# The Newton step of single-column inverse roots on GpSimd, and an output product that asks for no new weights

## The chip, the cores and the metric

The kernel runs on one core of a Trainium2 chip. The metric is the device time of one execution in microseconds (us); lower is better. Engines are called as in the profile: PE (TensorE matmuls), PEld (its weight loads), DVE (VectorE), ACT (ScalarE), POOL (GpSimd), SP (SyncE, which issues the DMAs here).

## The reference

Three blocks run one after the other on a sequence of 1024 positions of width 1024, all in float32: an attention block with a learned choice of 256 keys, a block of gated linear attention (GLA: 4 heads, head width 512 on the value side, chunks of 64), and a block with a state space model (S5), a gate and an output product; a last RMS norm ends it. What bears on this case is the inverse root of each norm, and the GLA head's way to the output:

```python
def _rmsnorm(x, g):
    y = x32 * lax.rsqrt(jnp.mean(x32 * x32, axis=-1, keepdims=True) + EPS) * g
...
    o = o_intra + jnp.einsum('bhncd,bhnde->bhnce', q_g, s_prev)
    o = o.transpose(0, 2, 3, 1, 4).reshape(bsz, seqlen, GLA_HEADS, GLA_DV)
    o = o * lax.rsqrt(jnp.mean(o * o, axis=-1, keepdims=True) + EPS) * head_gain.astype(f32)
    o = o.reshape(bsz, seqlen, D_INNER) * jax.nn.silu(z.astype(f32))
    return o.astype(h.dtype) @ w_out
```

## The kernel before, in words

All matmuls are float32 made of three products of "hi" and "lo" parts: `mm3` (lines 192 to 196) issues hi·hi, hi·lo and lo·hi into the same PSUM bank. Weights come from DRAM as raw pieces of 512 KB and are **split** on the chip: ACT casts the hi part (line 179), and DVE or POOL subtracts to get the lo part (line 187). A class `WStream` keeps the order: `put` lists the pieces, `pump(n)` splits up to n of the next ones, if the ring of six split pieces has room (`released + RING`) and if the raw piece's load was issued at least `age` pumps ago; `ahead` issues the loads of up to three raw pieces; `take(ids)` gives split pieces to a product, and splits at once, whatever the age, those that are not split yet; `release` gives ring places back.

**The inverse root.** `G.rsqrt` (line 204) takes a column of sums of squares. With up to four columns POOL makes v = mean + eps (line 211) and h = v to the power -0.5 (line 212); then one Newton step of four small DVE instructions (lines 215 to 218) gives the result. With `later=True` the Newton step is returned as a function, and the caller issues it some steps on. The single-column callers are: the norm of each of 8 row blocks at the end of the attention block (line 1325), each of the 32 items of the GLA core (line 1971), the 8 norms of the GLA result (line 2008), and the 8 last norms (`finish`, line 2447). The two calls with four columns, at the start, and those with more are not of this kind.

**The GLA core** (lines 2066 to 2089) goes through 32 items: 4 heads with 8 tiles of 128 positions each. Each item is a generator (`core`, line 1942) of five parts, and one turn of the loop, called a **round** here, advances the items under way in the order written in `turn` (line 2060), so that the instructions of a round stand in this order in every engine's queue:

1. the part 4 of item n-2: four PE transposes of y (line 1977) into a PSUM bank, ACT copy to hi (1982), DVE subtraction to lo (1983);
2. part 2 of item n-1: PE product with the state of the items before, DVE y = product times gate (1969), ACT squares with their sum (1970), POOL power (211, 212);
3. part 1 of item n: PE products, DVE new state `Sf` (1957), ACT `Shi` (1960), POOL `Slo` (1961 by line 187); the state is used by PE two rounds later;
4. part 3 of item n-1: the Newton step on DVE;
5. part 5 of item n-3: the output product, 24 matmuls of 512 columns with the head's four weight pieces (1992) into two banks, and then two DVE additions into `xacc` (1998), which multiply by the inverse root.

After that come two steps of `prep_unit`, which makes queries, keys and masks for the next four items; among its instructions are four PE transposes and 24 short matmuls (1920, 1930) in one round of four, an ACT copy and a POOL mask (1933). The round then ends with `ws.pump(1)` (line 2086). The name `mm` in the profile stands for four PSUM banks handed out in turn, so the transposes of the next round wait for a bank that the additions of line 1998 give back.

In a head's last tile (`last`, line 1989) the output product goes through the four weight pieces one after the other for both banks, releases each piece behind its use, and calls `ws.pump` there (line 1995): that puts the splits of the next pieces into the queues of ACT and DVE ahead of the additions of line 1998. A head's first tile takes its four pieces (line 1986) before its output product.

**The end of the kernel.** For each of the last four row blocks (lines 2530 to 2545): DVE adds the product, ACT squares, DVE adds two sums (2446), `rsqrt`, DVE scales twice (2450), and SP stores.

Of the kernel before, what the change touches and what calls it, by code (L numbers as in the profile page):

```python
# [16 lines left out]
OP = mybir.AluOpType  # L17
# [17 lines left out]
def f32(ap):  # L35
    return ap.bitcast(F)
# [110 lines left out]
class G:  # L147
# [56 lines left out]
    def rsqrt(self, pool, out, ssq, n, scale, later=False):  # L204

        nc = self.nc
        v = pool.tile([P, n], F, name=f"rs_v{n}", bufs=2 if n == 1 else 1)
        h = pool.tile([P, n], F, name=f"rs_h{n}", bufs=2 if n == 1 else 1)
        t = pool.tile([P, n], F, name=f"rs_t{n}", bufs=2 if n == 1 else 1)
        if n <= 4:  # L210
            nc.gpsimd.tensor_scalar(v, ssq, scale, EPS, op0=OP.mult, op1=OP.add)
            nc.gpsimd.tensor_tensor(h, v, self.mhalf[:, :n], OP.pow)  # L212

            def newton():
                nc.vector.tensor_tensor(t, h, h, OP.mult)  # L215
                nc.vector.tensor_tensor(t, t, v, OP.mult)  # L216
                nc.vector.scalar_tensor_tensor(t, t, -3.0, h, op0=OP.add, op1=OP.mult)
                nc.vector.tensor_scalar(out, t, -0.5, None, op0=OP.mult)
            return newton if later else newton()
        nc.vector.tensor_scalar(v, ssq, scale, EPS, op0=OP.mult, op1=OP.add)  # L220
        nc.vector.tensor_scalar(h.bitcast(I32), v.bitcast(I32), 1, None, op0=OP.logical_shift_right)
        nc.vector.tensor_scalar(out.bitcast(I32), h.bitcast(I32), -1.0, float(0x5F3759DF - 0x80000000),
                                op0=OP.mult, op1=OP.add)
        nc.vector.tensor_scalar(h, v, 0.5, None, op0=OP.mult)
        for _ in range(3):
            nc.vector.tensor_tensor(t, out, out, OP.mult)
            nc.vector.tensor_tensor(t, t, h, OP.mult)
            nc.vector.scalar_tensor_tensor(out, t, -1.5, out, op0=OP.add, op1=OP.mult)
# [1490 lines left out]
def gla(g, xn2, xstack, prep):  # L1719
    nc, tc, A, ws = g.nc, g.tc, g.A, g.ws  # L1720
# [221 lines left out]
    def core(h, st, v, z):  # L1942
        u = res[h, st // 4]
        p = st % 4
        sl = slice(p * P, (p + 1) * P)
        pk = g.big() if st < NST - 1 else None
        po = g.big()
        before = st8.get("S")
        if st < NST - 1:
            g.mm3(pk, [a[:, sl] for a in u["ke"]], v, True, True)  # L1950
        g.mm3(po, [a[:, sl] for a in u["am"]], v, True, st == 0)
        if st < NST - 1:
            Sf = wk2.tile([P, 512], F, name="Sf")
            if st == 0:
                nc.vector.tensor_copy(Sf, pk)
            else:
                nc.vector.scalar_tensor_tensor(Sf, before[0], u["dS"][:, p:p + 1], pk, op0=OP.mult, op1=OP.add)
            Shi = wk2.tile([P, 512], R, name="Shi")
            Slo = wk2.tile([P, 512], R, name="Slo")
            nc.scalar.copy(Shi, Sf)  # L1960
            g.sub("pool", Slo, Sf, f32(Shi))
            st8["S"] = (Sf, Shi, Slo)
        yield
        if st > 0:
            g.mm3(po, [a[:, sl] for a in u["qp"]], before[1:], False, True)
        ssq = wk2.tile([P, 1], F, name="ssq")
        rst = wk2.tile([P, 1], F, name="rsh", bufs=4)
        y = wk2.tile([P, 512], F, name="y")
        nc.vector.tensor_tensor(y, po, z, OP.mult)
        nc.scalar.activation(wk2.tile([P, 512], BF, name="sq", bufs=1), po, AF.Square, accum_out=ssq)  # L1970
        newton = g.rsqrt(wk2, rst, ssq, 1, 1.0 / 512, True)
        yield
        newton()
        yield
        ps = g.bank()
        for j in range(4):
            nc.tensor.transpose(ps[:, j * P:(j + 1) * P], y[:, j * P:(j + 1) * P], g.ident)
        wk2.tile([P, 32], F, name="ypad", bufs=1)
        yh = wk2.tile([P, 4, P], R, name="yh")
        yl = wk2.tile([P, 4, P], R, name="yl")  # L1980
        pv_ = ps.rearrange("p (a b) -> p a b", a=4)
        nc.scalar.copy(yh, pv_)
        nc.vector.tensor_tensor(yl, pv_, f32(yh), OP.subtract)
        yield
        if st == 0:
            st8["W"] = ws.take(pwo[h])
        ps = [g.bank(), g.bank()]
        cols = [slice(nh * 512, nh * 512 + 512) for nh in range(2)]
        last = st == NST - 1
        for i in range(8):  # L1990
            nh, j = (i % 2, i // 2) if last else (i // 4, i % 4)
            g.mm3(ps[nh], (yh[:, j], yl[:, j]), [a[:, 0, cols[nh]] for a in st8["W"][j]], j == 0, j == 3)
            if last and nh:
                ws.release(pwo[h][j:j + 1])
                ws.pump(j < 3)
        for nh in range(2):
            xs = xacc[:, st, cols[nh]]
            nc.vector.scalar_tensor_tensor(xs, ps[nh], rst, xs, op0=OP.mult, op1=OP.add)  # L1998
        if h == 3:
            nc.sync.dma_start(g.x3_d[st * P:(st + 1) * P, :], xacc[:, st, :])  # L2000
            norms.append(norm(st))
# [3 lines left out]
    def norm(st):  # L2005
        ss = g.small.tile([P, 2], F, name="nss", bufs=3)
        nc.scalar.activation(g.junk(), xacc[:, st, :], AF.Square, accum_out=ss[:, 0:1])
        newton = g.rsqrt(g.small, ss[:, 1:2], ss[:, 0:1], 1, 1.0 / D, True)
        yield
        yield  # L2010
        newton()
        yield
        nc.vector.tensor_scalar(xacc[:, st, :], xacc[:, st, :], ss[:, 1:2], None, op0=OP.mult)
# [52 lines left out]
    for n, (h, st) in enumerate(items):  # L2066
        if st % 4 == 0:
            for _ in pg:
                pass
            ui = n // 4 + 1  # L2070
            pg = pgs.pop(n, iter(()))
            if 0 < n and ui < len(units):
                pg = prep_unit(*units[ui], st8["next"])
        gens[n] = core(h, st, vs.pop(n), vz.pop(n)[1])
        if n + 1 < len(items):
            vs[n + 1] = split_v(vz[n + 1][0], "pool" if n % 2 else "dve")
        turn(n)
        next(pg, None)
        if n < 8 and n % 2 == 0:
            nc.sync.dma_start(xacc[:, n:n + 2], g.x2_d[n * P:(n + 2) * P].rearrange("(t p) d -> p t d", p=P))  # L2080
        if n + 3 < len(items):
            vz[n + 3] = load_vz(*items[n + 3])
        next(pg, None)
        if st % 4 == 1 and ui + 1 < len(units):
            st8["next"] = load(*units[ui + 1])
        ws.pump(1)
# [518 lines left out]
```

## Time and profile before

| | |
|---|---|
| median of 3 runs | 2616.41 us (2616.41 to 2618.24) |
| the profiled execution | 2615.66 us, span 2613.9 us, mean granted clock 0.964 |
| PE busy | 2417.1 us, 92% of the span |
| DVE busy | 1708.2 us, 65% |
| ACT busy | 1109.5 us, 42% |
| POOL busy | 1127.5 us, 43% |

The page gives busy time by engine, the span in forty slices, the chain of work that ended last, and groups of instructions by line. Times are counted from the first instruction. A bracket at the end of a row of the order in time, such as [5.55 <-DVE xacc L1998], is the engine's idle time before that instruction and what ended it. PE's busy time is modelled from pipelined matmuls; the distance between the starts of two matmuls is the better measure of its pace.

### The profile page before, as it was taken

The page shows a single profiled execution, that of the slowest core. Times are in us where ns is not written, and L with a number is a line of the kernel's source. Part 1 is how long each engine was busy: PE and PEld are TensorE (multiplying, and loading weights), DVE is VectorE, ACT ScalarE, POOL GpSimd, SP SyncE. Part 2 cuts the span into 40 slices and gives each one's busy share as a digit, 9 for nine tenths or more (in the row PEclk, how much of TensorE's full clock was granted, in tenths as well). Part 3 has the DMA queues.
Part 4 walks back from the last instruction along what each step waited for, and adds up shares of the span by engine and source line. Part 5 has one row for each costly group of instructions (what it writes and reads, how often), then busy time and mean ns, then how long its engine had stood idle before and what let it go on. Part 6 is the DMA issues. An engine that isn't in the chain of part 4 may idle for free.

```text
span 2613.9 us, 33041 instructions
## 1 busy us (share of the span) xinstructions
PE 2417.1 (92%) x11817; PEld 1990.4 (76%) x11817; DVE 1708.2 (65%) x3015; ACT 1109.5 (42%) x1812; POOL 1127.5 (43%) x826
## 2 busy tenths in 40 slices
PE   5787977999999999999989899999999899999998
PEld 4665755777777777777777678888888788888887
DVE  5889887777454556785777770389788555425642
ACT  5455683656532122324443443444443533323331
POOL 3517465322211566664444424555554433333431
PEclk8998988999999999999989899999999899999999
DMA  8302124221332645535432316777554644444441
GB/s 263 113 30 62 54 87 154 85 65 56 107 122 84 159 136 152 165 122 177 153 113 85 93 69 164 194 202 201 183 154 146 192 133 121 149 139 146 140 149 57
DMA packets 330173, 338.25 MB, mean 129 GB/s; under 512 B 67366, under 2 KB 248182, under 8 KB 329752
## 3 DMA queue, kind: packets, MB, share of 16 engines
q1 hardware_dynamic: 330008, 336.13, 42.2%
q8 instruction: 93, 1.52, 0.2%
q14 instruction: 72, 0.59, 0.1%
HBM read 239.19 MB, written 96.87 MB: 129 GB/s over the span
## 4 chain that ended last, share of the span: by engine, by line
PE 30%; DVE 10%; issue 5%; DMA 3%; POOL 3%; ACT 2%; SPq 0%; POOLq 0%; DVEq 0%; ACTq 0%
PE mm L194 8%; PE mm L196 8%; PE mm L195 8%; PE big L196 2%; PE big L195 2%; PE big L194 2%; POOL whl L187 2%; DMA w<-syp_d 2%; DVE xacc L1998 1%; DVE X L2326 1%; DVE rs_t L215 1%; DVE mm L2257 1%; POOL rs_h L212 1%; DVE mm L2255 1%; DVE rs_t L216 1%
## 5 line engine op out<-in xcount | busy, mean ns | idle before, releaser
L187 POOL TENSOR_TENSOR whl<-wraw,whl 128x1024 fp32r<-128x1024 f32 x183 | 443.3, 2431 | 606.0 <-ACT whl L179 527.3
L179 ACT CAST whl<-wraw 128x1024 fp32r<-128x1024 f32 (+1 forms) x279 | 288.5, 1048 | 360.9 <-PE mm L196 220.0
L194 PE MATMUL mm<-h_hi,whl 128*128 128x512 f32 x768 | 308.0, 401 | 14.5 <-DVE gT L952 7.8
L196 PE MATMUL mm<-h_hi,whl 128*128 128x512 f32 x768 | 302.0, 393 | 0.0
L195 PE MATMUL mm<-h_lo,whl 128*128 128x512 f32 x768 | 301.4, 392 | 0.0
L194 PE MATMUL mm<-whl,h_hi 128*128 128x512 f32 (+1 forms) x720 | 288.4, 400 | 13.0 <-ACT whl L179 9.6
L195 PE MATMUL mm<-whl,h_hi 128*128 128x512 f32 (+1 forms) x720 | 282.1, 392 | 10.8 <-DVE whl L187 10.8
L196 PE MATMUL mm<-whl,h_lo 128*128 128x512 f32 (+1 forms) x720 | 281.1, 390 | 0.0
L187 DVE TENSOR_TENSOR whl<-wraw,whl 128x1024 fp32r<-128x1024 f32 (+2 forms) x96 | 133.4, 1399 | 147.2 <-ACT whl L179 147.1
L194 PE MATMUL mm<-y_hl,whl 128*128 128x512 f32 x512 | 201.3, 393 | 0.0
L195 PE MATMUL mm<-y_hl,whl 128*128 128x512 f32 x512 | 199.9, 390 | 0.0
L196 PE MATMUL mm<-y_hl,whl 128*128 128x512 f32 x512 | 199.8, 390 | 0.0
L194 PEld LDWEIGHTS mm<-h_hi,whl 128*128 128x128 f32 x768 | 146.0, 190 | 49.5 <-DVE gT L952 8.7
L196 PEld LDWEIGHTS mm<-h_hi,whl 128*128 128x128 f32 x768 | 145.5, 189 | 32.2
L195 PEld LDWEIGHTS mm<-h_lo,whl 128*128 128x128 f32 x768 | 146.1, 190 | 29.4 <-issue 0.5
L194 PEld LDWEIGHTS mm<-whl,h_hi 128*128 128x128 f32 x720 | 137.7, 191 | 40.4 <-ACT whl L179 10.1
L195 PEld LDWEIGHTS mm<-whl,h_hi 128*128 128x128 f32 x720 | 138.0, 192 | 36.9 <-DVE whl L187 12.2
L196 PEld LDWEIGHTS mm<-whl,h_lo 128*128 128x128 f32 x720 | 137.3, 191 | 28.5
L187 POOL TENSOR_TENSOR w<-w 128x512 f32<-128x512 f32 x32 | 55.1, 1722 | 168.2 <-ACT w L2434 168.2
L196 PEld LDWEIGHTS mm<-y_hl,whl 128*128 128x128 f32 x512 | 96.5, 189 | 20.1
L194 PEld LDWEIGHTS mm<-y_hl,whl 128*128 128x128 f32 x512 | 97.0, 189 | 19.4
L195 PEld LDWEIGHTS mm<-y_hl,whl 128*128 128x128 f32 x512 | 96.6, 189 | 19.5
(542 smaller groups left out, 5928.8 us busy)
## 6 DMA issues: line engine op xcount, KB each, us to landing
wraw<-in_s_w_glu_dram SPq DMA_DIRECT2D x64, 512.0 KB, 3.9
wraw<-in_gla_w_in_dram SPq DMA_DIRECT2D x40, 512.0 KB, 4.3
wraw<-in_s_w_in_dram SPq DMA_DIRECT2D x32, 512.0 KB, 5.6
wraw<-in_s_w_out_dram SPq DMA_DIRECT2D x32, 512.0 KB, 3.6
gv_d<-stg SPq DMA_DIRECT2D x32, 256.0 KB, 2.2
v_mat<-vc SPq DMA_DIRECT2D x32, 256.0 KB, 2.6
w_mat<-wo SPq DMA_DIRECT2D x32, 256.0 KB, 2.5
gz_d<-stg SPq DMA_DIRECT2D x32, 256.0 KB, 2.1
```

The costliest lines, as they stand in the source:

```text
L179: nc.scalar.copy(out, in_)
L187: e.tensor_tensor(out, a, b, op)
L194: nc.tensor.matmul(out, lhsT=lhs[0], rhs=rhs[0], start=start, stop=False)
L195: nc.tensor.matmul(out, lhsT=lhs[0], rhs=rhs[1], start=False, stop=False)
L196: nc.tensor.matmul(out, lhsT=lhs[1], rhs=rhs[0], start=False, stop=stop)
L212: nc.gpsimd.tensor_tensor(h, v, self.mhalf[:, :n], OP.pow)
L215: nc.vector.tensor_tensor(t, h, h, OP.mult)
L216: nc.vector.tensor_tensor(t, t, v, OP.mult)
L1998: nc.vector.scalar_tensor_tensor(xs, ps[nh], rst, xs, op0=OP.mult, op1=OP.add)
L2255: nc.vector.tensor_tensor(a, x, wide(L[0], n), OP.mult)
L2257: nc.vector.tensor_tensor(c[half[q]], x[half[1 - q]], wide(L[1][half[1 - q]], n), OP.mult)
L2326: nc.vector.tensor_tensor(Xo.rearrange("p (g o) t -> p g t o", g=8), gto(parts.pop(o)), gto(ps), OP.add)
```

## The change

Two edits. In `rsqrt`, with one column, the Newton step is issued on POOL right behind the power, with four instructions (`h*h`, times v, times -0.5 plus 1.5, times h), and the function handed back does nothing. The formula is the same. In the last tile of a head the product no longer calls `ws.pump`; it still releases the pieces.

```diff
@@ -210,6 +210,12 @@
         if n <= 4:
             nc.gpsimd.tensor_scalar(v, ssq, scale, EPS, op0=OP.mult, op1=OP.add)
             nc.gpsimd.tensor_tensor(h, v, self.mhalf[:, :n], OP.pow)
+            if n == 1:
+                nc.gpsimd.tensor_tensor(t, h, h, OP.mult)
+                nc.gpsimd.tensor_tensor(t, t, v, OP.mult)
+                nc.gpsimd.tensor_scalar(t, t, -0.5, 1.5, op0=OP.mult, op1=OP.add)
+                nc.gpsimd.tensor_tensor(out, t, h, OP.mult)
+                return lambda: None
 
             def newton():
                 nc.vector.tensor_tensor(t, h, h, OP.mult)
@@ -1992,7 +1998,6 @@
             g.mm3(ps[nh], (yh[:, j], yl[:, j]), [a[:, 0, cols[nh]] for a in st8["W"][j]], j == 0, j == 3)
             if last and nh:
                 ws.release(pwo[h][j:j + 1])
-                ws.pump(j < 3)
         for nh in range(2):
             xs = xacc[:, st, cols[nh]]
             nc.vector.scalar_tensor_tensor(xs, ps[nh], rst, xs, op0=OP.mult, op1=OP.add)
```

## Rows read from the trace of the kernel before

**Rows 1.** Windows: length, then busy us (count) by engine, PEclk, DMA share, GB/s

```profile
1238.93:1553.72 314.79, 280.87 (x1311) 232.00 (x1311) 230.10 (x390) 125.14 (x246) 133.56 (x160) 0.92 0.32 105
1320.00:1325.00 5.00, 0.00 (x0) 0.00 (x0) 4.90 (x8) 2.92 (x5) 2.75 (x3) 0.69 0.74 227
1325.00:1330.00 5.00, 4.62 (x16) 3.88 (x17) 3.68 (x6) 1.51 (x4) 1.33 (x3) 0.63 0.77 267
```

**Rows 2.** Groups by line, 1235 to 1560: busy us, mean ns | idle before, releaser

```profile
L215 DVE TENSOR_TENSOR rs_t<-rs_h 128x1 f32<-128x1 f32 x40 | 28.8, 721 | 33.0 <-POOL rs_h L212 32.8
L216 DVE TENSOR_TENSOR rs_t<-rs_t,rs_v 128x1 f32<-128x1 f32 x40 | 18.6, 465 | 1.4
L217 DVE SCALAR_TENSOR_TENSOR rs_t<-rs_t,rs_h 128x1 f32<-128x1 f32 x40 | 16.6, 414 | 1.4
```

**Rows 3.** Waits, 1235 to 1560: us in total, times, longest

```profile
PE mm L1977 <- DVE xacc L1998: 22.7, 6, 6.1
```

**Rows 4.** PE in order of time: start, us, line, tiles, count, [idle before]

```profile
1308.30 0.60 PE L1977 MATMUL mm<-ident,y 128*128 128x128 f32 x4
...
1316.63 0.60 PE L1920 MATMUL mm<-ident,ek 128*128 128x128 f32 x4
...
1319.55 0.28 PE L196 MATMUL mm<-qgh,kkl 128*128 128x64 f32 x1
1325.38 1.12 PE L1977 MATMUL mm<-ident,y 128*128 128x128 f32 x4 [5.55 <-DVE xacc L1998]
...
1334.96 0.60 PE L1977 MATMUL mm<-ident,y 128*128 128x128 f32 x4
...
1342.92 0.60 PE L1977 MATMUL mm<-ident,y 128*128 128x128 f32 x4
...
1350.87 0.60 PE L1977 MATMUL mm<-ident,y 128*128 128x128 f32 x4
...
1365.07 1.11 PE L1977 MATMUL mm<-ident,y 128*128 128x128 f32 x4 [2.25 <-DVE xacc L1998]
...
1374.53 0.60 PE L1977 MATMUL mm<-ident,y 128*128 128x128 f32 x4
```

**Rows 5.** POOL and DVE in order of time at a head's last tile

```profile
1318.96 1.27 POOL L187 TENSOR_TENSOR Slo<-Sf,Shi 128x512 fp32r<-128x512 f32 x1
...
1319.02 1.22 DVE L215 TENSOR_TENSOR rs_t<-rs_h 128x1 f32<-128x1 f32 x1 [1.08 <-POOL rs_h L212]
...
1320.74 3.93 DVE L187 TENSOR_TENSOR whl<-wraw,whl 128x1024 fp32r<-128x1024 f32 x3
1324.59 1.40 DVE L1998 SCALAR_TENSOR_TENSOR xacc<-mm,rsh,xacc 128x512 f32<-128x512 f32 x2
```

**Rows 6.** ACT and DVE in order of time, around splits in other rounds

```profile
1339.00 0.62 ACT L1960 CAST Shi<-Sf 128x512 fp32r<-128x512 f32 x1
...
1346.78 1.05 ACT L179 CAST whl<-wraw 128x1024 fp32r<-128x1024 f32 x1
...
1347.86 1.47 DVE L187 TENSOR_TENSOR whl<-wraw,whl 128x1024 fp32r<-128x1024 f32 x1 [0.78 <-ACT whl L179]
```

**Rows 7.** POOL in order of time: first and last of another four-instruction Newton step

```profile
421.70 0.29 POOL L1043 TENSOR_TENSOR qrt<-qrs 128x64 f32<-128x64 f32 x1
...
422.82 0.33 POOL L1046 TENSOR_TENSOR qrs<-qrs,qrt 128x64 f32<-128x64 f32 x1
```

**Rows 8.** POOL and DVE in order of time, the last finish

```profile
2608.01 0.19 POOL L211 TENSOR_SCALAR rs_v<-fss 128x1 f32<-128x1 f32 x1 [4.69 <-DVE fss L2446]
2608.28 0.55 POOL L212 TENSOR_TENSOR rs_h<-rs_v,mhalf 128x1 f32<-128x1 f32 x1
...
2609.64 1.42 DVE L2450 SCALAR_TENSOR_TENSOR x<-x,frs,fn 128x512 f32<-128x512 f32 x2
```

**Rows 9.** POOL and DVE in order of time, end of the GLA stage

```profile
1549.46 2.35 POOL L187 TENSOR_TENSOR whl<-wraw,whl 128x1024 fp32r<-128x1024 f32 x1
...
1549.58 2.25 DVE L216 TENSOR_TENSOR rs_t<-rs_t,rs_v 128x1 f32<-128x1 f32 x1
```

## The prediction, made before the change was built

> **What bounds the kernel now.** PE is busy 92% of the span, so a change on DVE, POOL and ACT can only pay where PE stands still or runs at the lower clock. I read the windows first, to find such places. In the GLA core, 314.8 us long, PE is busy 280.9 us and the mean granted clock is 0.92 [rows 1]. The loss is not spread: in 1320 to 1325 PE does nothing, and the next 5 us run at a granted clock of 0.63, that is for much of the time at 1.2 instead of 2.4 GHz [rows 1]. The view of waits says what PE stood for: the transposes of line 1977 waited 22.7 us in six stops for DVE's additions into `xacc` [rows 3], which give their PSUM bank back. Then I read PE in order of time, round by round [rows 4]. A round without a stop lasts 1350.87 - 1342.92 = 7.95 us. In one round of four the short products of `prep_unit` come on top, from 1316.63 to about 1319.66, 3.0 us, so that round should last 10.95 us. At the end of a head it lasted 1325.38 - 1308.30 = 17.08 us, 6.13 too long, and the round behind it 9.58 us, 1.63 too long, because its first part ran at the low clock. In the middle of a head the same two rounds lasted 14.20 and 9.46 us, so 3.25 and 1.51 are lost [rows 4]. Each kind occurs three times: 3 x 7.76 = 23.3 us at the ends of heads, 3 x 4.76 = 14.3 us in the middles.
>
> Why are the additions late? The groups by line show that the small Newton instructions do not cost their 0.16 us here: the three with two inputs take 0.72, 0.47 and 0.41 us on average, and DVE stands idle another 33.0 us ahead of them for POOL's power [rows 2]. In order of time the reason is to be seen: line 215 begins at 1319.02, behind POOL's `Slo` that began at 1318.96, and ends when `Slo` ends [rows 5]. At the end of a head, idle time and Newton step hold DVE from 1317.94 to 1320.74, 2.8 us, and then three splits hold it to 1324.59; only then come the additions, and PE goes on at 1325.38 [rows 5, 4].
>
> **The Newton step leaves DVE.** In the core it takes 28.8 + 18.6 + 16.6 us of DVE and 33.0 us of waiting in 40 calls [rows 2], some 2.4 us a round. With it gone, the additions come right behind `Sf`, or when the product ends. In the middle of a head PE's transposes waited 2.25 us for them [rows 4], less than the 2.8 us of idle time and Newton step ahead of the additions at the head's end [rows 5], and the rounds before lag less as well. I take these three stops as gone: -14.3 us. Less than all is bounded by the DVE work that stays; none of it gone would be 0.
>
> On POOL the same step costs this: another Newton step there, with 64 columns, took 421.70 to 423.15, 1.45 us, 0.29 to 0.33 us for an instruction with two inputs [rows 7]. With one column a POOL instruction is 0.19 us and the next begins 0.27 us after it [rows 8], so four take 0.08 + 3 x 0.27 + 0.19 = 1.08 us. That is the value I take; 1.5 us is the upper end, and the 0.81 us that DVE needs from the end of the power to line 2450 [rows 8] the lower. POOL is busy 133.6 of 314.8 us in the core [rows 1], 4.2 us a round; 5.3 fits into 7.95. Queued behind the step on POOL are `Slo`, the mask and the lo parts of v. `Slo` is used two rounds later, the inverse root two rounds later, the mask a round later, so 1.08 us is hidden. Only the first mask of the stage has no such slack; there I add 1.1 us (0 to 1.5).
>
> The Trainium skill, page "GPSIMD Engine Reference", section 4.1 "Engine selection", advises against this edit: adding and multiplying belongs on VectorE, since GpSimd is about twice as slow with two inputs. By it each of the three such instructions would take 2 x 0.16 = 0.32 us instead of 0.19, an estimate from that page, and a finish would lose 0.4 us more. The rows with one and with 64 columns are 0.19 and about 0.3 us [rows 7, 8], so the start of an instruction sets the time and I keep to the rows. The Trainium skill's page "SBUF — State Buffer", section "SBUF: two separate sides", says that DVE instructions with two SBUF inputs and GpSimd instructions exclude each other for a whole instruction. Line 215 beside `Slo` agrees [rows 5]. By that rule the new step on POOL can in turn be held by a split on DVE (1.3 us each in rows 5), which the slack of a round covers.
>
> **The ends of heads.** Without the pumps the three splits, 3.85 us of DVE, leave their place ahead of the additions, and with the Newton step's 2.8 us the additions would begin 6.65 us earlier, at 1317.94. PE's short products last until about 1319.66, so the stop is gone: -23.3 us. But the splits do not vanish. At a head's last tile the ring holds two pieces of the next head. The third is now split by the pump that ends the round. The fourth is not split until `take` asks for it in the next round, immediately ahead of the product that needs it. ACT has it behind `Shi` and DVE behind `Sf`. Measured on the round that begins at 1334.96 [rows 4]: a round of 7.95 us has 33 matmuls of 512 columns and four short transposes, so 0.23 us for a matmul; nine of them and the transposes come first, so the product begins at about 1337.5, and the fourth piece is wanted nine matmuls or 2.0 us later, at 1339.5. `Shi` ends at 1339.62, the cast takes 1.05, to 1340.7, and the subtraction 1.05 to 1.47, to 1341.7 or 1342.2 [rows 6]: PE waits 2.0 to 2.5 us. The split of the third piece stands ahead of that round's `yh` on ACT and can add 1.05. I take 2.7 us, and the slow clock behind it (1.5 us) in half of the cases: 3.4 us, 10.3 us for three heads. The lower end is 0 (DVE is earlier in all rounds now), the upper the old price, 23.3. The first piece of the head after next was split in the head's last tile too; it moves to the pump of the next round, where only its place in a queue changes. At the end of the last head there is one split that goes into the S5 stage. It is on POOL at 1549.46 and holds DVE's line 216 for 2.25 us [rows 9], which delays the last additions and PE's first S5 transposes. Without it 2.25 - 0.16 = 2.1 us go, the Newton step on POOL gives 0.3 back: -1.8 us. In S5 the piece is wanted by the third projection only.
>
> **The last norms.** In `finish` the step lies on the path: POOL's 1.08 us and a hop replace DVE's 0.81, so a finish is 0.3 us longer [rows 8]. The last four stand one behind another on DVE: +1.25 us (0.3 if only the last counts, 3 at 1.5 us a step). In the attention block eight norms free DVE of 0.8 us and bring ACT's scaling 0.3 us later: 0, between -2.5 and +2.5.
>
> **The sum.** -14.3 - 23.3 + 10.3 + 1.1 - 1.8 + 1.25 = -26.8 us. The profiled execution took 2615.66 us, so 2588.9; the median of the runs is 0.75 above it, so I predict 2590 us.
>
> **Rivals.**
> 1. *The fourth piece takes the stop over.* Its split is a new wait on the same two queues, and if DVE lags in that round, or PE's clock falls each time, it costs what the old stop did. For it: PE idles of 2.25 us did lower the clock here [rows 4]. Against: one split of 1.3 us is behind it, not three. -26.8 + 13 = -13.8: 2603 us.
> 2. *It costs nothing,* because without the Newton steps `Sf`, `Shi` and the split run ahead of PE. Against: `Sf` cannot begin before PE's products of the same round, 0.7 us ahead of the output product. -37.1: 2579 us.
> 3. *POOL becomes the bound; slower than before.* Place: POOL's queue in the core; price: the four instructions, each held by DVE or slow in itself. POOL has 4.2 us a round; the round was 314.8 / 32 = 9.84 on average, so the core is slower than before from 5.6 us a call, 1.4 us an instruction. At 1.6 us POOL takes 10.6 us a round: +24 us, and +22 in the last four finishes: 2662 us. The nearest rows have 0.19 to 0.33 us [rows 7, 8].
> 4. *The edit does not free PE.* The additions are only the last of several late things, and ACT's copies or PE's own order keep the stops: 2612 to 2619 us. Against: the six stops all ended with line 1998 [rows 3].
>
> **How the numbers follow.** Forecast 0.62, rival 1 0.17, rival 2 0.13, rivals 3 and 4 0.04 each. About 0.2% (5 us) is what a measurement of this kernel can tell from no change. The forecast and rivals 1 and 2 lie all beyond it on the fast side: faster 0.92, same 0.04, slower 0.04. The range goes from rival 2 with the attention block's better end, 2576, to rival 1 with the worse ends of the last norms and the attention block, 2607.
>
> **What would show it.** In the profile after: no Newton instruction of one column on DVE, lines of POOL at 0.19 us in their place; in the core a granted clock near 1 and rounds of 7.95 and 10.95 us; the waits of line 1977 for line 1998 near 0; in the first round behind a head's end, a wait of PE's output product (line 194 or 195) for a split of line 179 or 187; the last `finish` 0.3 us longer from the power to line 2450. The prediction is wrong if PE's stops in the middles of heads stay, if the new wait is above 5 us, or if POOL's four instructions take over 2 us.

## The result, and the profile after

The changed kernel takes 2584.81 us (median of four runs, 2580.13 to 2585.3), the kernel before beside it 2617.32 us (2616.41 to 2621.31). The ratio is 0.9867, with a 95% interval of 0.9856 to 0.9879 (the two medians divided give 0.9876). The profiled execution took 2584.43 us. Forecast were 2590 us, in a range of 2576 to 2607.

The edits add six lines above `core`, so its lines are numbered six higher (1977 is 1983, 1982 is 1988); from the place of the removed pump on they are five higher (1998 is 2003). The Newton instructions on POOL have lines 214 to 217.

Windows of the kernel after, with the columns of [rows 1]: the core from its first transposes to its last, and the two stretches of 5 us that stood in [rows 1]. The core from first to last transposes was 302.59 us long before.

```profile
1236.85:1510.73 273.88, 260.53 (x1264) 215.56 (x1265) 166.37 (x230) 123.47 (x244) 168.36 (x303) 0.98 0.36 121
1320.00:1325.00 5.00, 2.40 (x11) 1.43 (x9) 3.31 (x5) 3.48 (x6) 3.75 (x6) 1.00 0.55 175
1325.00:1330.00 5.00, 5.00 (x24) 4.15 (x25) 2.24 (x4) 1.25 (x3) 1.45 (x2) 1.00 0.13 50
```

The granted clock has risen from 0.92 to 0.98. Behind the head's end (1325 to 1330) PE is busy all the time at a granted clock of 1.00, where [rows 1] had 0.63.

PE in order of time, the answer to [rows 4]:

```profile
1306.13 0.60 PE L1983 MATMUL mm<-ident,y 128*128 128x128 f32 x4
1317.14 0.65 PE L1983 MATMUL mm<-ident,y 128*128 128x128 f32 x4
1323.73 0.49 PE L194 MATMUL mm<-whl,yh 128*128 128x512 f32 x1 [1.84 <-ACT whl L179]
1324.99 0.50 PE L195 MATMUL mm<-whl,yh 128*128 128x512 f32 x1 [0.77 <-DVE whl L187]
1328.31 0.60 PE L1983 MATMUL mm<-ident,y 128*128 128x128 f32 x4
1336.29 0.60 PE L1983 MATMUL mm<-ident,y 128*128 128x128 f32 x4
1344.27 0.60 PE L1983 MATMUL mm<-ident,y 128*128 128x128 f32 x4
1355.27 0.65 PE L1983 MATMUL mm<-ident,y 128*128 128x128 f32 x4
1362.59 0.60 PE L1983 MATMUL mm<-ident,y 128*128 128x128 f32 x4
```

No transposes wait for additions any more. The round that ends a head lasts 11.01 us (17.08 before), and the one behind it 11.17, with the new wait in two pieces: for the hi part of the fourth piece, and then for its lo part. In the middle of a head the two rounds last 11.00 and 7.32 us (14.20 and 9.46 before).

The Newton step in the core, the answer to [rows 2], and its instructions in the last finish, the answer to [rows 8]:

```profile
L214 POOL TENSOR_TENSOR rs_t<-rs_h 128x1 f32<-128x1 f32 x40 | 8.9, 222 | 3.1
L215 POOL TENSOR_TENSOR rs_t<-rs_t,rs_v 128x1 f32<-128x1 f32 x40 | 8.2, 204 | 3.1
L216 POOL TENSOR_SCALAR rs_t<-rs_t 128x1 f32<-128x1 f32 x40 | 10.8, 271 | 3.5
```

```profile
2576.49 0.55 POOL L212 TENSOR_TENSOR rs_h<-rs_v,mhalf 128x1 f32<-128x1 f32 x1
2577.12 0.19 POOL L214 TENSOR_TENSOR rs_t<-rs_h 128x1 f32<-128x1 f32 x1
...
2577.94 0.19 POOL L217 TENSOR_TENSOR frs<-rs_t,rs_h 128x1 f32<-128x1 f32 x1
2578.17 1.42 DVE L2455 SCALAR_TENSOR_TENSOR x<-x,frs,fn 128x512 f32<-128x512 f32 x2 [2.04 <-POOL frs L217]
```

They take 0.20 to 0.27 us on average on POOL, where three of them took 0.41 to 0.72 us on DVE, and the 33 us of DVE's waiting for the power are gone. In the finish, 2577.04 (end of the power) to 2578.17 is 1.13 us, against 0.81.

### The profile page after: what moved, and what is told of

It is laid out like the page before. It is cut to its first block, busy times and chain, and to the rows that moved or that the text cites. A ratio compares the mean times of both kernels' runs of the same rounds, so it can differ in the third digit from the quotient of the medians.

```text
span 2582.5 us, 33062 instructions
## 1 busy us (share of the span) xinstructions
PE 2408.6 (93%) x11817; PEld 1985.8 (77%) x11817; DVE 1641.0 (64%) x2791; ACT 1109.2 (43%) x1812; POOL 1180.7 (46%) x1050
## 4 chain that ended last, share of the span: by engine, by line
PE 30%; DVE 6%; DMA 6%; issue 5%; POOL 4%; SPq 2%; ACT 1%; POOLq 0%; DVEq 0%; ACTq 0%
PE mm L195 8%; PE mm L196 8%; PE mm L194 8%; POOL whl L187 3%; PE big L196 2%; PE big L194 2%; PE big L195 2%; DMA w<-syp_d 2%; DMA wraw<-kp_d 1%; SPq L100 1%; DMA wraw<-w_mat 1%; DVE X L2331 1%; DVE mm L2262 1%; DVE mm L2260 1%; DVE mm L2284 0%
```

## The experiments

Theories at the start. The first, as in the prediction: the Newton step on DVE, with its wait for the power, and the splits ahead of the additions made the stops together, and what is left is the wait for the fourth piece. Rivals: one edit does it all; it is not the wait for the power but DVE's instructions beside POOL's that cost; POOL is near its limit. Each run below was timed in five rounds beside the kernel before, whose medians (15 or 16 runs) were 2618.8, 2619.16 and 2618.75 us in the three groups of four runs.

**The Newton step on POOL alone.** The changed kernel, with the pump put back:

```diff
             if last and nh:
                 ws.release(pwo[h][j:j + 1])
+                ws.pump(j < 3)
```

> Newton step on POOL, pumps of the last tile kept. Theory (DVE's queue ahead of the additions of line 1998 stops PE; a piece split at the last moment costs 3.1 us at each of three heads): the middles of heads keep their whole gain, rounds of 11.0 and 7.3 us. At a head's end three splits (3.85 us) stand ahead of the additions, but not the Newton step (2.8 us): PE idles about 2.9 us instead of 5.55, some 4 us lost a head instead of 7.8, and no wait for the fourth piece; about 1 us a head worse than both edits. At the end of the GLA stage the split on POOL is back, ahead of the last additions: +2 to +4. So 2588 to 2592 us, against 2584.8 for both edits. Rival (the pumps were the larger cost): the stops at the ends of heads come back whole, 2600 us or more.

Measured: 2588.42 us (2586.44 to 2590.71), ratio 0.988 (0.9867 to 0.9894). This is within the theory's range. At the ends of heads the old stop is there in a shorter form, and the next transposes run at the low clock (granted 0.50 from 1318.0 to 1319.5):

```profile
1304.32 0.60 PE L1983 MATMUL mm<-ident,y 128*128 128x128 f32 x4
1318.00 1.12 PE L1983 MATMUL mm<-ident,y 128*128 128x128 f32 x4 [2.53 <-DVE xacc L2004]
1327.57 0.60 PE L1983 MATMUL mm<-ident,y 128*128 128x128 f32 x4
```

The two rounds last 23.25 us here, 24.41 and 22.19 at the other two heads, against 26.66 to 27.20 before and 22.09 to 22.18 with both edits. Almost all of the gain is this edit's: 30.4 of 32.5 us by the medians.

**The pump alone.** The kernel before, with the pump taken out and nothing else:

```diff
                 ws.release(pwo[h][j:j + 1])
-                ws.pump(j < 3)
```

> Newton step on DVE as before, no pumps in the last tile. Theory: the stops in the middles of heads stay whole (16 to 17 us lost); at a head's end the additions come 3.85 us earlier, PE idles 1.9 us instead of 5.55, but the fourth piece is split behind a DVE that still has the Newton steps, 3 to 5 us; so a head gains 0 to 2 us. The end of the GLA stage gains 2. 2606 to 2614 us, in any case less than a third of the gain of both edits. Rival (the pumps were the larger cost): 2600 us or less.

Measured: 2619.17 us (2615.66 to 2621.41), ratio 1.0 (0.9991 to 1.0009). All theories missed: no gain is left to be seen. At a head's end the old stop shrinks and the new one comes on top:

```profile
1310.33 0.60 PE L1977 MATMUL mm<-ident,y 128*128 128x128 f32 x4
1323.54 0.66 PE L1977 MATMUL mm<-ident,y 128*128 128x128 f32 x4 [1.69 <-DVE xacc L1997]
1332.31 0.51 PE L195 MATMUL mm<-whl,yh 128*128 128x512 f32 x1 [1.92 <-DVE whl L187]
1335.61 0.60 PE L1977 MATMUL mm<-ident,y 128*128 128x128 f32 x4
```

25.28 us for the two rounds here, 26.23 and 27.81 at the other two heads. This is the prediction's rival 1 as it would have come without the first edit: as long as DVE carries the Newton step it is late in the next round too, and the split that moved there holds PE just as long. In the trace the six rounds at the ends of heads are 1.4 us shorter in sum and the end of the GLA stage 2.0, but the core's last five rounds are 2.5 us longer, with a wait of 2.02 us for y, and the part behind is 2.8 us longer; whether that is the edit's doing no run shows. So the two edits don't add up: the second gives nothing alone and 3.6 us on top of the first, by medians whose intervals against the kernel before overlap.

**Newton on DVE, but later.** The kernel before without the pump, and the same four DVE instructions issued a round later, behind `yl`, when the power is long there:

```diff
-        newton()
...
         nc.vector.tensor_tensor(yl, pv_, f32(yh), OP.subtract)
+        newton()
...
-                ws.pump(j < 3)
```

> No pumps in the last tile; in the core the Newton step stays on DVE, but is issued one round later, behind the item's yl, where its inputs are long there; elsewhere as before. It separates the two costs of the step on DVE: waiting for POOL's power (33 us in 40 calls) and standing beside POOL's instructions (0.72, 0.47 and 0.41 us in place of 0.16). If the waiting stopped PE: rounds as with both edits, 7.95 and 11 us, and 2582 to 2588 us, the last norms being 1.3 us shorter than with both edits. If standing beside POOL's instructions was the cost: Newton instructions of over 0.4 us on average again, stops in the middles of heads of 2 us or more, 2593 to 2605 us.

Measured: 2601.91 us (2601.47 to 2602.63), ratio 0.9932 (0.992 to 0.9945). That lies in the second theory's range, but neither of its signs came: no Newton instruction takes over 0.4 us on average, and the stops in the middles of heads are gone (11.10 and 7.32 us). DVE waits 2.2 us for the power instead of 33.0. The groups of the Newton step, and PE behind a head's end:

```profile
L215 DVE TENSOR_TENSOR rs_t<-rs_h 128x1 f32<-128x1 f32 x40 | 13.0, 324 | 2.2 <-POOL rs_h L212 2.2
L216 DVE TENSOR_TENSOR rs_t<-rs_t,rs_v 128x1 f32<-128x1 f32 x40 | 12.7, 317 | 1.4
```

```profile
1324.07 0.79 PE L194 MATMUL mm<-whl,yh 128*128 128x512 f32 x1 [2.92 <-ACT whl L179]
1325.83 0.80 PE L195 MATMUL mm<-whl,yh 128*128 128x512 f32 x1 [0.96 <-DVE whl L187]
```

Here PE waits 2.92 us for the fourth piece, the next matmuls run at the low clock (granted 0.54 from 1326 to 1331), and the two rounds last 25.98 us, against 22.2 with the step on POOL. So a step on DVE need not stop PE in the middles of heads, if it doesn't stand right ahead of the additions. The run doesn't part the two costs that it set out to part: with the wait for the power (33.0 to 2.2 us) half of the time of the three instructions went too (64.0 to 32.1 us). What is left of the step on DVE, about 1 us a round ahead of y and the splits, is paid at the ends of heads; that is how the trace reads, and no run shows it alone.

**The fourth piece split in time.** The changed kernel, with one split right behind the additions of a head's last tile:

```diff
             nc.vector.scalar_tensor_tensor(xs, ps[nh], rst, xs, op0=OP.mult, op1=OP.add)
+        if last and h < 3:
+            ws.pump(1)
```

> Both edits, and for heads 0 to 2 one pump more, behind the additions of the last tile, so that the third and the fourth piece are both split in the round of the head's end, and take finds them ready. Theory: the wait of the output product in the next round (1.84 and 0.77 us, 3.1 us with the restart) goes at three heads: -9.3 us, 2575 us. Rival (the two splits behind the additions delay yh and yl of the next round and PE waits there instead): 2581 to 2585 us.

Measured: 2574.04 us (2571.33 to 2578.46), ratio 0.9827 (0.9813 to 0.984), as the theory had it. The wait for the fourth piece is gone, and the two rounds last 19.01 us:

```profile
1307.05 0.60 PE L1983 MATMUL mm<-ident,y 128*128 128x128 f32 x4
1318.04 0.66 PE L1983 MATMUL mm<-ident,y 128*128 128x128 f32 x4
1326.06 0.60 PE L1983 MATMUL mm<-ident,y 128*128 128x128 f32 x4
```

So the split was not wrong in the last tile, only ahead of the additions; the new wait was a real cost of the change, 3 x 3.1 us.

**The last norms back on DVE,** on top of that: `rsqrt` gets a switch.

```diff
-            if n == 1:
+            if n == 1 and not dve:
...
-        g.rsqrt(qpool, rst, ss[:, 2:3], 1, 1.0 / D)
+        g.rsqrt(qpool, rst, ss[:, 2:3], 1, 1.0 / D, dve=True)
```

> The changed kernel with the one split behind the additions at the heads' ends, and with the Newton step of the eight last norms back on DVE. Theory (each of the last four finishes lost 0.32 us to POOL's step, one behind another on DVE): 4 x 0.32 = 1.3 us less than the kernel with the split alone (2574.0), so 2572.8. Rival (only the very last one counts): 0.3 us less, 2573.7. Either way the distance from the end of the power to the scaling on DVE should be 0.8 us again in the trace, where the changed kernel has 1.13.

Measured: 2571.85 us (2567.7 to 2577.57), ratio 0.982 (0.9805 to 0.9835). The distance from the power to the scaling is 0.81 us again, and a finish lasts 5.52 us instead of 5.82. In the trace the edit is worth 4 x 0.3 us; the medians differ by 2.2, and their intervals overlap.

**The first item on DVE too,** on top of that:

```diff
-        newton = g.rsqrt(wk2, rst, ssq, 1, 1.0 / 512, True)
+        newton = g.rsqrt(wk2, rst, ssq, 1, 1.0 / 512, True, h == 0 and st == 0)
```

> The kernel of the last norms on DVE, and the Newton step of the first item of the GLA core back on DVE too. Theory (the stage's start is 2.0 us longer because POOL makes the first Newton step ahead of the first mask): 1 to 2 us less than the kernel without this edit, 2571 to 2572, and 17.7 us from the first product of the core to the fourth transposes, where the changed kernel has 19.7. Rival (the start is late for another reason, the load of the second item's values, which came last there): no difference, 2572.8.

Measured: 2573.07 us (2569.14 to 2573.97), ratio 0.982 (0.9807 to 0.9833): no difference. The second transposes come 8.13 us behind the first instead of 9.20, which is the 1.07 us of the step, but the third come 10.48 us behind the second instead of 9.41, so both kernels need 18.61 us for the two. ACT's `vh` of that stretch ended a wait for the DMA of `lv` in both kernels; whether that alone takes the time back stays open.

**The GLA result's norms on DVE:** the changed kernel, with the switch at this call alone.

```diff
-        newton = g.rsqrt(g.small, ss[:, 1:2], ss[:, 0:1], 1, 1.0 / D, True)
+        newton = g.rsqrt(g.small, ss[:, 1:2], ss[:, 0:1], 1, 1.0 / D, True, True)
```

> The changed kernel with the Newton step of the eight norms of the GLA result back on DVE. The end of the GLA stage became 4.9 us shorter, where 1.8 was forecast. Theory A (the split that no longer stands there, and additions that come earlier in the rounds before, made it shorter; on which engine these eight steps are is worth some tenths): from the last transposes of the core to the first product of the S5 block 17.8 to 19 us, as in the changed kernel (18.3), and 2584 to 2586 in all. Theory B (these eight steps held DVE there, behind the power): 20 us or more, 2587 to 2589.

Measured: 2585.86 us (2581.62 to 2589.4), ratio 0.9876 (0.9862 to 0.989). From the last transposes to the first product of S5 18.94 us, against 18.30 in the changed kernel and 23.15 before: theory A. These eight steps are worth 0.6 us of the 4.9. The first two runs divide the rest: 20.40 us with the first edit alone, 21.16 with the second alone.

**The Newton step twice.** The changed kernel with the four POOL instructions issued twice, same result:

```diff
                 nc.gpsimd.tensor_tensor(out, t, h, OP.mult)
+                nc.gpsimd.tensor_tensor(t, h, h, OP.mult)
+                nc.gpsimd.tensor_tensor(t, t, v, OP.mult)
+                nc.gpsimd.tensor_scalar(t, t, -0.5, 1.5, op0=OP.mult, op1=OP.add)
+                nc.gpsimd.tensor_tensor(out, t, h, OP.mult)
```

> The changed kernel with the four POOL instructions of the Newton step issued twice, with the same result: 1.08 us more on POOL for each of the 48 calls. Theory (POOL has slack in the core; its step is on the path only at the stage's start, at its end and in the last four finishes): the core's rounds stay at 7.3, 8.0 and 11.0 us; +4 x 1.08 = 4.3 in the finishes, +1 to 2 at the start and end of the GLA stage: 2590 to 2592. Rival (POOL's queue already sets the core's pace, as in the prediction's case that ends slower than before): +1.08 a round, +35 us in the core: 2620 or more.

Measured: 2621.41 us (2612.7 to 2627.82), ratio 1.0008 (0.9998 to 1.0018): the whole gain of the change is gone. The rival of this run was right in its total but not in its place, since it put 35 us into the core, and the prediction's word that the step "is hidden" hangs by a thread. The core from first to last transposes is 294.62 us, 20.7 more; of the rest 4.3 are at the end of the GLA stage, 4.4 in the last four finishes, 5.3 in S5 (not followed up) and 1.7 ahead of the core. Some 17 of the 20.7 us in the core fall into the preparing rounds and those behind them, the rest into its first and last rounds. POOL, then DVE and PE, in one of them:

```profile
1276.48 0.55 POOL L212 TENSOR_TENSOR rs_h<-rs_v,mhalf 128x1 f32<-128x1 f32 x1
...
1279.56 0.19 POOL L221 TENSOR_TENSOR rsh<-rs_t,rs_h 128x1 f32<-128x1 f32 x1
1279.70 1.29 POOL L187 TENSOR_TENSOR Slo<-Sf,Shi 128x512 fp32r<-128x512 f32 x1
1280.93 0.40 POOL L1922 COPY enb<-ek 128x256 f32<-128x256 f32 x1
```

```profile
1281.37 0.43 DVE L1924 TENSOR_TENSOR ek<-ek,ebl 128x256 f32<-128x256 f32 x1 [2.77 <-POOL enb L1922]
1282.97 1.48 DVE L187 TENSOR_TENSOR whl<-wraw,whl 128x1024 fp32r<-128x1024 f32 x1 [1.18 <-ACT whl L179]
1284.37 0.68 DVE L187 TENSOR_TENSOR vl<-lv,vh 128x512 fp32r<-128x512 f32 x1
1284.97 0.68 DVE L1993 TENSOR_TENSOR yl<-mm,yh 128x512 fp32r<-128x512 f32 x1
...
1285.70 0.30 PE L194 MATMUL mm<-qgh,kgh 128*128 128x64 f32 x1 [1.51 <-DVE yl L1993]
```

The columns are those of [rows 5]. Behind the Newton step in POOL's queue stand `Slo` and then instructions of `prep_unit`: here the copy into `enb`, a round earlier the first `ek`. ACT and DVE, which work in order, wait for them (ACT 3.49 us for `enb`), and behind these waits stand the weight split, `yl` and the next y. The short products of the round then wait for the PSUM bank that `yl` gives back.

**The Newton step four times.** The same four lines three times over, sixteen instructions in all.

> The changed kernel with the four POOL instructions issued four times: 3.24 us more on POOL for each call. POOL has 173.4 us of busy time in the 292 us of the core, 5.4 us a round; it would have 8.7, against rounds of 8.0 (11.0 with the preparing products), 8.7 on average. Theory (slack, then a bound): the finishes take 4 x 3.24 = 13 us more, the start and end of the GLA stage 3 to 6; the core is at the edge of being bound by POOL, 0 to 20 us more: 2601 to 2624, with waits for POOL's tiles in the core. Rival (POOL's place in the queue counts from the first instruction on, so each added 3.24 us comes out in full in 32 rounds): +104 in the core and +17 outside, 2705.

Measured: 2725.56 us (2722.99 to 2727.17), ratio 1.0404 (1.039 to 1.0418): above both theories. The core is 67.4 us longer than in the changed kernel, between the theory's 0 to 20 and the rival's 104. The same waits have grown:

```profile
ACT ek L1911 <- POOL ek L1910: 38.1, 6, 7.2
ACT kkh L1920 <- POOL enb L1930: 33.8, 6, 5.7
```

In the changed kernel these two are 14.2 and 12.1 us in six times each. A step more costs 1.08 x 6 = 6.5 us in each line; (38.1 - 14.2) / 3 = 8.0 and (33.8 - 12.1) / 3 = 7.2 come near.

**Two instructions more.** The changed kernel with the first two issued twice, 1.62 us a step:

```diff
+                nc.gpsimd.tensor_tensor(t, h, h, OP.mult)
+                nc.gpsimd.tensor_tensor(t, t, v, OP.mult)
                 nc.gpsimd.tensor_tensor(t, h, h, OP.mult)
```

> The changed kernel with two more POOL instructions in each single-column step (h*h and times v issued twice, same result): 1.62 us a step instead of 1.08, a little above the upper end of 1.5 that the prediction set. Theory (POOL is full in one round of four, 7.5 to 7.8 us busy of 7.98, and there each further tenth shows at once): 0.2 to 0.5 us in each of seven preparing rounds, +2 to 4 in the core; the finishes, early and late, 8 x 0.54 = 4.3; 2590 to 2594. Rival (there is slack of more than half a microsecond everywhere in the core): +0 in the core, 2587 to 2589.

Measured: 2596.12 us (2593.81 to 2597.88), ratio 0.9916 (0.9903 to 0.9928), 11.3 us more than the changed kernel and above both theories. The core is 5.6 us longer, the end of the GLA stage 1.3, and 3.6 lie behind it, 2.2 of them in the last four finishes. The preparing rounds have reached the edge:

```profile
1281.09 0.30 PE L194 MATMUL mm<-qgh,kgh 128*128 128x64 f32 x1 [0.66 <-DVE yl L1991]
```

**Another place for POOL's value splits.** The doubled step, with `vl` made on POOL in rounds 0 and 3 of four:

```diff
-            vs[n + 1] = split_v(vz[n + 1][0], "pool" if n % 2 else "dve")
+            vs[n + 1] = split_v(vz[n + 1][0], "pool" if n % 4 in (0, 3) else "dve")
```

> The kernel with the Newton step issued twice, and POOL's share of the value splits dealt out otherwise: the lo part of v is made on POOL in rounds 0 and 3 of four instead of 1 and 3, so that POOL has 1.28 us less in its full round and as much more in its empty one; the number of instructions on each engine stays the same. Theory (what the doubled step cost in the core is that one full round in four): of the 20.7 us that the core was longer at least half goes, 2600 to 2610. Rival (the doubled step costs by POOL's load on average, or by its delay in every round): no difference, 2618 to 2624.

Measured: 2625.93 us (2620.31 to 2634.21), ratio 1.0029 (1.0017 to 1.0041). Nothing comes back, and the core is as long as with the doubled step alone, 294.59 us: my theory of the full round did not come true. POOL now has idle time in that round, and PE waits longer:

```profile
1281.66 0.19 POOL L211 TENSOR_SCALAR rs_v<-ssq 128x1 f32<-128x1 f32 x1 [2.62 <-ACT sq L1980]
```

```profile
1277.83 1.77 DVE L187 TENSOR_TENSOR vl<-lv,vh 128x512 fp32r<-128x512 f32 x1
1279.52 0.68 DVE L1993 TENSOR_TENSOR yl<-mm,yh 128x512 fp32r<-128x512 f32 x1
...
1290.58 0.68 DVE L1993 TENSOR_TENSOR yl<-mm,yh 128x512 fp32r<-128x512 f32 x1
...
1291.31 0.30 PE L194 MATMUL mm<-qgh,kgh 128*128 128x64 f32 x1 [1.87 <-DVE yl L1993]
```

POOL waits 2.62 us for the squares, so it is not out of time. But `Slo` and `ek` still stand behind the Newton step, and the value split that left POOL now stands right ahead of a `yl` on DVE (1277.83), in the chain itself; the `yl` that PE waits for is the next one, at 1290.58. So the run took load off POOL and put it on DVE, and the two could cancel. What the doubled step costs is a chain round the engines: y, the squares on ACT, power and Newton step, `Slo` and `ek` or `enb` on POOL, the casts of ACT, `yl` and the next y on DVE. That is how the traces read, and POOL's idle time in this run speaks against its load as the cause; a run that takes only `ek` and `enb` out of the step's shadow was not made.

**The control:** the same dealing out, in the kernel with the split behind the additions and the last norms on DVE.

> The kernel with the split behind the additions and the last norms on DVE, with the same dealing out of the value splits, as the control: there POOL's full round has 7.5 us busy of 8 and PE had no wait in the core. Theory (a round that is not yet full costs nothing): no difference, 2570 to 2574. Rival (POOL's full round delays PE in this kernel too, unseen in the waits): 2 us or more faster, 2567 to 2570.

Measured: 2571.08 us (2569.55 to 2574.97), ratio 0.9824 (0.9812 to 0.9837): no difference from 2571.85, as expected. These two are the fastest kernels of the study, some 13 us below the changed one.

## Why the prediction was right, step by step

- **Mid-head stops, -14.3 forecast:** gone, as said. Three times 18.32 us for the two rounds, against 24.16, 23.66 and 23.80: -16.7. The term was too small mainly because the round behind lasts 7.32 us when nothing stops it, not the 7.95 taken from another round [rows 4]. The reason given, idle time and Newton step right ahead of the additions, held: with the step on DVE but a round later the stops went too. How much of it is the wait and how much the instructions beside POOL's was not parted.
- **Ends of heads, -23.3 + 10.3 = -13.0 forecast:** -14.4 measured (66.36 us against 80.72 for three). The new wait came where it was placed, in two pieces of 1.84 and 0.77 us, and costs 22.18 - 19.01 = 3.2 us a head, against 3.4. Its parts were off: PE stood 2.6 us, not 2.7, and no clock fall followed (granted clock 1.00 in 1325 to 1330), where half of one was counted; in its place, each of the two matmuls that had to wait takes 0.5 us alone, where the flow goes on every 0.23 us. That no clock fell is luck: with the GLA result's norms on DVE, where the same two waits stand (1.73 and 0.76 us), it fell at one head of three, and the two rounds there took 1.6 us longer than at the others, near the 1.5 us of the prediction. The prediction counted both edits in this term together and did not ask what each brings: the pump alone brings nothing, and its rival 1, the stop taken over by the fourth piece, is what happens then.
- **First mask of the stage, +1.1 forecast:** +2.0 measured, 19.72 against 17.74 us from the first transposes to the third. The second transposes win back 1.07 us when the first item's step is on DVE, but the third do not. The stretch also varies by itself: in four other traces with the changed kernel's code there it took 18.51 to 19.22 us, and 18.46 with the pump alone, which has the code of before. By the means, 18.92 and 18.10 us, 0.8 of the 2.0 us is the step's.
- **End of the GLA stage, -1.8 forecast:** -4.9 measured. The split's part is 20.40 - 18.30 = 2.1, as forecast. What failed is the sign of the other part: the Newton step on POOL was booked as 0.3 us lost, and it brought 23.15 - 20.40 = 2.75. The eight norms of the GLA result are 0.6 of that; the rest goes with the step of the core's items, which no run took apart.
- **Last norms, +1.25 forecast:** 0.32 a finish, and the last four are 1.3 us longer in all.
- **Attention, 0 forecast:** the core's first transposes come 1.6 us later, within the bounds of 2.5. Four other traces with the same code up to there have them between 1231.81 and 1238.36, so 1.6 us cannot be told from nothing.
- **The sum:** the span fell by 31.4 us, against 26.8; the two terms that were too small, 2.4 at the mid-heads and 3.1 at the stage's end, and 1.4 at the ends of heads make up more than the difference, and 0.9 and 1.6 at the starts take the rest back. The median came 5 us below the forecast partly because these errors have different signs.
- **Rival 3, POOL as the bound,** was placed rightly as the one on the slower side and sized wrongly. It was said to turn the kernel slower from 5.6 us a call, by POOL's busy time per round. The runs put that point at 2.2 us (2621 us), and 1.62 us, just above the upper end taken for the step, already cost 11 us. The step that failed is the list of what stands behind the Newton step: "`Slo`, the mask and the lo parts of v" leaves out `ek` and `enb` of `prep_unit`, for which ACT waits in order. In the changed kernel's trace six preparing rounds lie 0.5 to 1.4 us from the edge: `yl` begins 1.21 to 2.16 us ahead of the short products that need its bank, and where PE waits for it that distance is 0.73 us.

```profile
1279.56 0.68 DVE L1989 TENSOR_TENSOR yl<-mm,yh 128x512 fp32r<-128x512 f32 x1
...
1280.85 0.28 PE L194 MATMUL mm<-qgh,kgh 128*128 128x64 f32 x1
```

So "1.08 us is hidden" was true with half a microsecond to spare, and not with the 7.95 - 5.3 = 2.65 us of the prediction's average. Even that is not sure in each execution. The run with the Newton step on POOL alone has the changed kernel's code up to the first head's end, and in the first of these rounds its distance was 0.73 us: PE waited 0.19 us, the round behind ran at a granted clock of 0.81, and the two rounds took 20.37 us instead of 18.32. With the last norms on DVE they took 20.29.

## What to carry to other kernels

A small instruction costs what stands behind it in its queue: before moving one, list everything issued behind it on the new engine, in each kind of round, and follow the waits until they reach PE; a mean busy time per round says little about that slack. Two edits at one stop need not add up, so size the second only with the first in place. And when a piece of work is late, look for the slot just behind the critical instruction before moving it a whole round on.

## What the runs showed of the hardware

- Single-column instructions on POOL are not always 0.19 us. Beside a split on DVE one lasts as long as the split:

```profile
1507.28 1.23 DVE L187 TENSOR_TENSOR whl<-wraw,whl 128x1024 fp32r<-128x1024 f32 x1 [2.22 <-ACT whl L179]
1507.29 1.27 POOL L214 TENSOR_TENSOR rs_t<-rs_h 128x1 f32<-128x1 f32 x1
```

This is [rows 5] with the roles changed, as the prediction allowed for. It agrees with the Trainium skill, page "SBUF — State Buffer", section "SBUF: two separate sides": whichever of a DVE instruction with two SBUF inputs and a GpSimd instruction that reads SBUF starts first keeps the shared port for its whole length. It is rare in the changed kernel, where the means of these instructions are 0.20 to 0.27 us.

- A stop of PE does not always lower its clock, and these traces do not show what decides. 1.84 and 0.77 us of waiting, 0.5 us of work apart, left the granted clock at 1.00 in the next 5 us. With the GLA result's norms on DVE 1.75 and 0.76 us did so at two heads, but behind 1.73 and 0.76 us at the third the matmuls came 0.43 us apart instead of 0.23 (granted clock 0.72 from 1322 to 1328). With Newton on DVE, but later, 2.92 us was followed by a matmul of 0.79 us at two heads and of 0.49 at the other, and with the step on POOL alone 2.53 us by transposes of 1.12 us instead of 0.60.
